# A row scale moved from the up products to the down products of a squared-ReLU MLP

## The chip, the cores and the metric

The kernel runs on one core of one Trainium2 chip. The core has a matrix engine (TensorE, PE in the profile; its weight loads are listed apart as PEld), VectorE (DVE), ScalarE (ACT), GpSimd (POOL), and SyncE (SP), which here only issues transfers. All five run their own instruction streams in order and wait for one another by semaphores. Matrix products land in PSUM, eight banks of 512 float32 per partition; everything else works in SBUF, 128 partitions wide. The metric is the device time of one execution in microseconds (us), lower is better.

## The reference

One layer of a streaming encoder on 512 tokens of width 1024, float32. After two attention-like blocks have been added to the residual `h`, the MLP and the final norm follow:

```
def rmsnorm(x, g):
    y = x * rsqrt(mean(x * x, axis=-1) + EPS)
    return y * g

u = rmsnorm(h, norm_ff_g) @ w1        # 1024 -> 4096
h = h + square(relu(u)) @ w2          # 4096 -> 1024
out = rmsnorm(h, final_norm_g)
```

The norm multiplies each token (row of `h`) by one positive number r and each feature by a gain. A positive factor per row passes through the product with `w1` and through relu, and comes out of the square as r squared; the product with `w2` keeps it as a factor of the row. So r may be applied on `u`, or r squared on the rows of the product with `w2`.

## The kernel before, in words

**Precision.** Every operand of a product is split into a high and a low part (`hi`, `lo`) by one ACT copy and one DVE subtraction, and each product runs as three: hi x hi, lo x hi, hi x lo (lines 240 to 242 for the up products, 1367 to 1369 for the down products). Weights come by transfer into raw buffers (`wr`, two of them, for the up weights; `wq` for the down weights), then ACT writes the high part (`whu`, `whd`, line 175) and DVE the low part (`wlu`, `wld`, line 179). Four buffers of each part rotate.

**Order of the work.** PE's order is written by hand: it is the program's order. The orders of ACT, DVE and POOL come from a planner that simulates the program by priority, which is program order, with weight splits put back by a fixed offset (`PW`). In the closing part (`last_product`) ACT and DVE are written by hand too.

**The residual before the MLP.** `residual` (line 1044) runs the output projection of the cross attention (`xw`) feature block by feature block, eight blocks of 128 features by 512 tokens. For each block DVE adds the product to the residual (`hT`), ACT and DVE write `x2_hi` and `x2_lo` with the gain applied (lines 1068 and 1069), and POOL squares the block and adds it to `ssq` (lines 1071 to 1075). Behind blocks 2, 4 and 6, and again in the MLP, `to_tok` transposes finished blocks on PE (`ht`, line 1167) and copies them into `acc`, four tiles of 128 tokens by 1024 features, to which the MLP's result is added.

**The MLP.** The 4096 hidden features go in eight groups of 512. For a group, `mlp_up` makes four tiles `u` of 128 hidden features by 512 tokens, 24 matmuls each, in PSUM banks that rotate among three (`mm`). `square` takes each: DVE computes `ur` = max(u, 0) times the row scale (line 1303, the scale broadcast to all partitions in `rbc`), and ACT squares it into `sq` (line 1306). `hidden_sums` (lines 1312 to 1315) forms sums and differences for a scheme of seven products in place of eight, and `hidden_part` splits those (`hb`). `mlp_down` runs the seven products in the order 1, 2, 6, 5, 7, 3, 4 into banks U, V, U, Y, U, Y, U, each twice, once for each half of the tokens. Bank U is accumulated further by products 6, 7 and 4, and bank Y by product 3, so that after each product the bank's present content is added to `acc` with a sign by `add_to` on DVE (lines 1333 and 1335) before PE may write it again. Down products of group g-1 run behind the up products of group g; the last down stretch takes groups 6 and 7 together. The last addition (line 1413) stands in `last_product`, in two halves of 256 columns.

**The scale before.** At the start of the MLP, after the first up tile, `mean_sq` sums `ssq` over the features on PE (`pm`, line 1085), POOL makes r by a power of -0.5, and after the second up tile PE broadcasts r over all partitions (`rbc`, line 1505), DVE copies it, and only then are the first two tiles squared:

```
    up0 = next(ups)
    ms2 = mean_sq(ssq2, "pm2")
    r2 = rstd_of(ms2, NT, "r2")
    to_tok(KC - 2)
    to_tok(KC - 1)
    up1 = next(ups)
```

Of the kernel before, what the change touches and what calls it, by code (L numbers as in the profile page):

```python
# [9 lines left out]
F32 = mybir.dt.float32  # L10
R = mybir.dt.float32r
U8 = mybir.dt.uint8
AF = mybir.ActivationFunctionType
ALU = mybir.AluOpType
AX = mybir.AxisListType

P = 128
S = 512
NT = S // P
D = 1024  # L20
KC = D // P
# [6 lines left out]
EPS = 1e-6  # L28
# [14 lines left out]
def emit(  # L43
# [22 lines left out]
    te, ve, ac, gp = nc.tensor, nc.vector, nc.scalar, nc.gpsimd  # L66
# [5 lines left out]
    cp = ctx.enter_context(tc.tile_pool(name="cp", bufs=1))  # L72
# [23 lines left out]
    def k4(shape, name, dt=F32):  # L96
        return k4p.tile([P] + shape, dt, tag="k4", name=name)
# [7 lines left out]
    def t2(name, dt=F32, shape=(S,)):  # L105
        return t2p.tile([P] + list(shape), dt, tag="t2", name=name)

    def sm(n, name):
        if n > 8:
            return s3p.tile([P, n], F32, tag="s3", name=name, padded_shape=[P, 32])  # L110
        return smp.tile([P, n], F32, tag="sm", name=name, padded_shape=[P, 8])
# [10 lines left out]
    def tr(name, shape=(S,)):  # L122
        return trp.tile([P] + list(shape), F32, tag="tr", name=name)
# [194 lines left out]
    ident = cp.tile([P, P], F32, name="ident")  # L318
# [24 lines left out]
    rows = t2("rows", F32, (P,))[0:33, :]  # L343
# [14 lines left out]
    def rstd_of(ms, n, name, r=None):  # L358

        e = sm(n, name + "e")  # L360
        gp.tensor_scalar(e, ms, 1.0, EPS, op0=ALU.mult, op1=ALU.add)
        if r is None:
            r = sm(n, name)
        gp.tensor_tensor(r, e, mhalf[:, 0:n], op=ALU.pow)
        return r
# [76 lines left out]
    with tc.manual_schedule(engines={mybir.EngineType.Activation, mybir.EngineType.DVE}):  # L442
# [66 lines left out]
        gf2 = gemm_fm(gfps[2], wt1, 0, hn_hi, hn_lo)  # L509
        for _ in range(GF):  # L510
            next(gf2)
        r0 = cp.tile([P, NT], F32, name="r0")
        rstd_of(ms0, NT, "r0", r0)

        fb = cp.tile([P, FH], F32, name="fb")
# [2 lines left out]
        pb = sc("rbc")  # L518
        for tb in range(NT):
            te.matmul(pb[:, tb * P : (tb + 1) * P], r0[:, tb : tb + 1].to_broadcast([P, P]), ident, start=True, stop=True)  # L520
        rbc = cp.tile([P, S], F32, name="rbc")
# [41 lines left out]
    g_x, g_mem, g_ff, g_h = gv[:, 0:8], gv[:, 8:16], gv[:, 16:24], gv[:, 24:25]  # L563
    gate(3)
    forget(3)
    for hp in range(2):
        wt = next_panel()
        for j in range(2):
            h = 2 * hp + j
            ps = mm(f"gq{h}")  # L570
# [124 lines left out]
    for li, m in enumerate(mlev):  # L695
# [8 lines left out]
        for hp in range(2):  # L704
# [3 lines left out]
            ps = sc(f"lv{hp}{m}", (NT, 2, w))  # L708
# [123 lines left out]
    for c in range(NT):  # L832
# [24 lines left out]
        with ahead(P1):  # L857
            hs = sm(4, f"hs{c}")
            for h in range(4):
                j = t2(f"hj{c}{h}", F32, (P,))  # L860
# [134 lines left out]
    for n in range(len(pairs) + 2):  # L995
        if n < len(pairs):
            p, tb = pairs[n]
# [46 lines left out]
    def residual(src_hi, src_lo, g, dst_hi, dst_lo, name, ssq, order, nlast, after=None):  # L1044

        ps_, gens = {}, {}

        def open_(c):
            if c % 2 == 0:
                open_.wt = next_panel()  # L1050
            ps_[c] = mm(f"{name}{c}")
            gens[c] = gemm_fm(ps_[c], open_.wt, (c % 2) * P, src_hi, src_lo, order=order)

        def early():

            for c in range(3):
                open_(c)
                for _ in range(KC - nlast):
                    yield next(gens[c])

        def rest():
            for c in range(KC):
                if c not in gens:
                    open_(c)
                yield from gens[c]
                hc = hTc(c)
                ve.tensor_tensor(hc, hc, ps_[c], ALU.add)  # L1067
                ac.activation(dst_hi[:, c, :], hc, AF.Identity, scale=g[:, c : c + 1])  # L1068
                ve.scalar_tensor_tensor(dst_lo[:, c, :], hc, g[:, c : c + 1], f(dst_hi[:, c, :]), op0=ALU.mult, op1=ALU.subtract)
                if c == 0:  # L1070
                    gp.tensor_tensor(ssq, hc, hc, op=ALU.mult)
                else:
                    sq = t2(f"{name}sq{c}")
                    gp.tensor_tensor(sq, hc, hc, op=ALU.mult)
                    gp.tensor_tensor(ssq, ssq, sq, op=ALU.add)
                if after is not None and c in (2, 4, 6):
                    after(c - 2)
                    after(c - 1)

        return early, rest  # L1080

    def mean_sq(ssq, name):
        pm = tr(name, (NT,))
        for tb in range(NT):
            te.matmul(pm[:, tb : tb + 1], ssq[:, tb * P : (tb + 1) * P], ones, start=True, stop=True)
        ms = sm(NT, name + "m")
        ve.tensor_scalar(ms, pm, 1.0 / D, None, op0=ALU.mult)
        return ms
# [8 lines left out]
    o_hi, o_lo = act_tile("o_hi"), act_tile("o_lo")  # L1097
# [14 lines left out]
    run_now(x_proj(0))  # L1112
    ms1 = mean_sq(ssq1, "pm1")
    r1 = rstd_of(ms1, NT, "r1")
    r16 = cp.tile([P, NT], F32, name="r16")
    gp.tensor_scalar(r16, r1, 1.0 / 16.0, 0.0, op0=ALU.mult, op1=ALU.add)

    def x_scores(h, tp):
# [43 lines left out]
    acc = []  # L1162
# [14 lines left out]
    for h in range(4):  # L1177
        if 0 < h < 3:
            fill.add(x_proj(h + 1), f"xq{h + 1}")
        elif h == 3:  # L1180
            x2_hi, x2_lo = act_tile("x2_hi"), act_tile("x2_lo")
            ssq2 = t2("ssq2")
            early, rest = residual(o_hi, o_lo, g_ff, x2_hi, x2_lo, "xw", ssq2, range(KC), 2, to_tok)
            fill.add(early())
        x_scores(h, 0)
        fill.run(X1)
        x_scores(h, 1)
        fill.run(X2 + X3)
        x_T_(h, 0)
        x_T_(h, 1)  # L1190
        pth, ptl = s4([2, S], f"pth{h}", R), s4([2, S], f"ptl{h}", R)
        for mc in range(2):
            ac.activation(pth[:, mc, :], xpT[h][mc], AF.Copy)
            ve.tensor_tensor(ptl[:, mc, :], xpT[h][mc], f(pth[:, mc, :]), ALU.subtract)
        if h < 3:
            fill.until(f"xq{h + 1}")
        else:
            fill.run(X4)
        x_out(h, pth, ptl)
# [99 lines left out]
            yield g, j, i, ps  # L1299

    def square(g, j, i, ps):
        u = t2(f"ur{g}{j}{i}")
        ve.scalar_tensor_tensor(u, ps, 0.0, rbc2, op0=ALU.max, op1=ALU.mult)  # L1303
        if i == 0:
            sqs[g, j] = k4([2, S], f"sq{g}{j}")
        ac.activation(sqs[g, j][:, i, :], u, AF.Square)  # L1306

    def hidden_sums(g):
        qa, qb = sqs[g, 0], sqs[g, 1]
# [18 lines left out]
        hbs[g, name] = hb  # L1328

    def add_to(ps, rows, half, t, sign):  # L1330
        a = acc[2 * rows + t][:, half * S : (half + 1) * S]
        if sign > 0:
            ve.tensor_tensor(a, ps, a, ALU.add)
        else:
            ve.scalar_tensor_tensor(a, ps, -1.0, a, op0=ALU.mult, op1=ALU.add)


    PLAN = {
# [42 lines left out]
    def last_product(gs, banks):  # L1381

        name = PRODUCTS[-1]

        def steps(g, t, cols):
            (whi, wlo), hb = unit("d", g, name), hbs[g, name]
            for k in range(2):
                hi, lo = (hb[:, x, k, t * P : (t + 1) * P] for x in range(2))
                yield from ((hi, whi[:, k, cols]), (hi, wlo[:, k, cols]), (lo, whi[:, k, cols]))

        def product(ps, t, cols, start):
            ops = [op for g in gs for op in steps(g, t, cols)]
            for i, (a, b) in enumerate(ops):
                te.matmul(ps, a, b, start=start and i == 0, stop=i == len(ops) - 1, skip_group_check=True)

        with tc.manual_schedule(engines={mybir.EngineType.Activation, mybir.EngineType.DVE}):
            add_to(banks["U", 1], 1, 0, 1, 1)
            product(banks["U", 0], 0, slice(0, S), False)
            add_to(banks["U", 0], 1, 0, 0, 1)
            o2, o3, v = s4([D], "fo2"), s4([D], "fo3"), fin[3][0]  # L1400
            _, half1, o1, r1_ = deferred
            scale_a(1, o1, r1_)
            e2 = sm(1, "fv2")
            ac.activation(o2[:, 0:S], acc[2][:, 0:S], AF.Square, scale=1.0 / 32.0, accum_out=e2)
            gp.tensor_tensor(e2, e2, fin[2][0], op=ALU.add)
            r2_ = row_scale(e2, "fr2")
            dma_a(1, o1)
            scale_b(1, half1, o1, r1_, gfin[half1])
            for q in range(2):
                qs = slice(q * HS, (q + 1) * HS)  # L1410
                ps = mm(f"Z{q}")[:, 0:HS]
                product(ps, 1, qs, True)
                ve.tensor_tensor(acc[3][:, qs], ps, acc[3][:, qs], ALU.add)
                v = squares(3, o3, qs, v, f"fv3{q}")
            for tb, o, r in ((2, o2, r2_), (3, o3, row_scale(v, "fr3"))):
                scale_a(tb, o, r)
                dma_a(tb, o)
                scale_b(tb, 0, o, r, gfin_ps)
# [73 lines left out]
    down_units((NG - 2, NG - 1))  # L1492
    order = [k for k, _ in unit_q]

    rbc2 = rbc
    ups = mlp_up_group(0)
    up0 = next(ups)
    ms2 = mean_sq(ssq2, "pm2")
    r2 = rstd_of(ms2, NT, "r2")
    to_tok(KC - 2)  # L1500
    to_tok(KC - 1)
    up1 = next(ups)
    pb = tr("rbc2")
    for tb in range(NT):
        te.matmul(pb[:, tb * P : (tb + 1) * P], r2[:, tb : tb + 1].to_broadcast([P, P]), ident, start=True, stop=True)
    ve.tensor_copy(rbc2, pb)
    square(*up0)
    square(*up1)
    for up in ups:
        square(*up)  # L1510
    hidden_sums(0)
# [43 lines left out]
```

## Time and profile before

| | |
|---|---|
| runs | 768.29, 768.75, 768.94 us (median 768.75) |
| profiled execution, first to last instruction | 766.8 us, the only time given for it |
| PE busy | 757.8 us, 99%, 4085 matmul instructions, clock granted in full |
| DVE busy | 525.2 us, 68% |
| ACT busy | 366.8 us, 48% |
| POOL busy | 193.6 us, 25% |
| MLP on PE | from 430.5 us to 759.9 us |

The profile is one execution. Its page gives the busy share of each engine and the chain of work that ended last, followed back from the last instruction to whatever released each step. The groups of instructions name line, engine, operation, output and inputs, shape and count; after the bar stand the busy time in us and the mean duration of one in ns, after the next bar the engine's idle time just before them and what ended it. The timeline gives for each instruction its start and duration in us, and in brackets the idle time before it and its releaser. The matmuls of PE overlap: one of 512 columns is listed with 0.39 us, but the next starts 0.23 us after it. An instruction of PE in full float32 shows as two, so that four transposes are listed as eight.

### The profile page before, as it was taken

How to read it: one execution, taken by the hardware profiler on the slowest of the kernel's cores; microseconds unless marked ns; L12 is line 12 of the kernel's file. 1: busy time of each engine (PE TensorE's matmuls, PEld its weight loads, DVE VectorE, ACT ScalarE, POOL GpSimd, SP SyncE). 2: the span in 40 equal slices, each digit the busy share in tenths (PEclk: the TensorE clock that was granted, in tenths of full speed). 3: DMA queues.
4: the chain of work that ended last, by engine and by line, in shares of the span. 5: the costliest groups of instructions: out<-in, count | busy, mean ns of one | idle time of the engine just before them, and what ended most of it. 6: DMA issues, size and time to landing. Idle time of an engine off the chain costs nothing.

```text
span 766.8 us, 10952 instructions
## 1 busy us (share of the span) xinstructions
PE 757.8 (99%) x4085; PEld 638.0 (83%) x4085; DVE 525.2 (68%) x848; ACT 366.8 (48%) x617; POOL 193.6 (25%) x264
## 2 busy tenths in 40 slices
PE   9999999999999999999999999999999999999996
PEld 6889888888889988888888888888888888888885
DVE  5747863678877656565548566949596877777696
ACT  5655554656666523344444344435353534343553
POOL 7207531322542225310016510101011010101123
PEclk9999999999999999999999999999999999999999
DMA  8541333313535432231113695575758475758602
GB/s 247 193 129 56 95 84 111 111 56 111 194 115 175 136 124 83 89 99 61 56 56 109 210 257 138 147 173 161 178 151 202 140 185 146 193 138 220 136 1 110
DMA packets 78870, 103.01 MB, mean 134 GB/s; under 512 B 4657, under 2 KB 56410, under 8 KB 78818
## 3 DMA queue, kind: packets, MB, share of 16 engines
q1 hardware_dynamic: 69266, 76.61, 31.2%
q0 software_dynamic: 8960, 24.67, 15.3%
q10 hardware_dynamic: 592, 1.05, 0.4%
q8 instruction: 32, 0.52, 0.3%
q14 instruction: 20, 0.16, 0.1%
HBM read 89.71 MB, written 4.21 MB: 122 GB/s over the span
## 4 chain that ended last, share of the span: by engine, by line
PE 95%; DVE 2%; ACT 1%; POOL 1%; issue 1%; ACTq 0%; POOLq 0%
PE u L241 8%; PE u L242 8%; PE u L240 8%; PE U L1368 4%; PE U L1369 4%; PE U L1367 4%; PE xq L240 2%; PE wo L240 2%; PE xq L241 2%; PE xw L240 2%; PE xq L242 2%; PE xw L241 2%; PE wo L241 2%; PE xw L242 2%; PE wo L242 2%; PE Y L1368 2%
## 5 line engine op out<-in xcount | busy, mean ns | idle before, releaser
L179 DVE TENSOR_TENSOR wld<-wq,whd 128x1024 fp32r<-128x1024 f32 x56 | 68.4, 1222 | 24.8 <-ACT whd L175 24.7
L240 PE MATMUL u<-x_hi,whu 128*128 128x512 f32 x192 | 74.7, 389 | 0.0
L241 PE MATMUL u<-x_lo,whu 128*128 128x512 f32 x192 | 74.7, 389 | 0.0
L242 PE MATMUL u<-x_hi,wlu 128*128 128x512 f32 x192 | 74.7, 389 | 0.0
L175 ACT ACTIVATE whd<-wq 128x1024 fp32r<-128x1024 f32 x56 | 58.4, 1052 | 30.5 <-PE u L241 21.6
L175 ACT ACTIVATE whu<-wru 128x1024 fp32r<-128x1024 f32 x24 | 25.3, 1053 | 61.2 <-DMA wru<-in_w_dram 61.2
L1243 POOL DMA_DIRECT2D wq<-in_w_dram x16 | 19.4, 1242 | 130.3 <-DMA wq<-in_w_dram 118.9
L179 DVE TENSOR_TENSOR wlu<-wru,whu 128x1024 fp32r<-128x1024 f32 x24 | 29.3, 1220 | 32.0 <-ACT whu L175 32.0
L1367 PE MATMUL U<-whd,hb 128*128 128x512 f32 x120 | 46.7, 389 | 0.0
L1368 PE MATMUL U<-wld,hb 128*128 128x512 f32 x120 | 46.7, 389 | 0.0
L1369 PE MATMUL U<-whd,hb 128*128 128x512 f32 x120 | 46.7, 389 | 0.0
L1243 POOL DMA_DIRECT2D wq<-wq x16 | 14.1, 878 | 122.7 <-DVE wld L179 95.9
L240 PEld LDWEIGHTS u<-x_hi,whu 128*128 128x128 f32 x192 | 36.0, 188 | 7.5
L241 PEld LDWEIGHTS u<-x_lo,whu 128*128 128x128 f32 x192 | 36.0, 188 | 7.5
L242 PEld LDWEIGHTS u<-x_hi,wlu 128*128 128x128 f32 x192 | 36.0, 188 | 7.4
L925 POOL TENSOR_SCALAR bi<-nF,Ft 128x128 f32<-128x128 f32 (+3 forms) x32 | 22.7, 718 | 58.2 <-PE pt L957 33.4
L1306 ACT ACTIVATE sq<-ur 128x512 f32<-128x512 f32 x32 | 20.0, 625 | 27.0 <-DVE ur L1303 27.0
L1303 DVE SCALAR_TENSOR_TENSOR ur<-u,rbc 128x512 f32<-128x512 f32 x32 | 21.9, 687 | 13.0 <-PE u L242 13.0
L1367 PEld LDWEIGHTS U<-whd,hb 128*128 128x128 f32 x120 | 22.5, 188 | 4.7
L1368 PEld LDWEIGHTS U<-wld,hb 128*128 128x128 f32 x120 | 22.5, 188 | 4.7
L1369 PEld LDWEIGHTS U<-whd,hb 128*128 128x128 f32 x120 | 22.5, 188 | 4.7
L1068 ACT ACTIVATE x_hi<-hT,gv 128x512 fp32r<-128x512 f32 x16 | 11.5, 716 | 30.4 <-DVE hT L1067 30.4
(961 smaller groups left out, 2311.7 us busy)
## 6 DMA issues: line engine op xcount, KB each, us to landing
wq<-in_w_dram SPq DMA_DIRECT2D x40, 512.0 KB, 3.3
wru<-in_w_dram SPq DMA_DIRECT2D x24, 512.0 KB, 6.7
wq<-in_w_dram POOLq DMA_DIRECT2D x16, 512.0 KB, 8.2
wq<-wq POOLq DMA_DIRECT2D x16, 512.0 KB, 4.7
xTd<-xT POOLq DMA_DIRECT2D x4, 512.0 KB, 3.3
nF<-Fd POOLq DMA_DIRECT2D x8, 256.0 KB, 3.8
hT<-xTd POOLq DMA_DIRECT2D x4, 512.0 KB, 5.6
xt<-in_x_dram SPq DMA_DIRECT2D x3, 512.0 KB
```

The lines of the kernel that those rows point to most:

```text
L175: ac.activation(hi, raw, AF.Copy)
L179: ve.tensor_tensor(lo, raw, f(hi), ALU.subtract)
L240: te.matmul(ps, wh, hi, start=n_ == 0 and not begun, stop=False)
L241: te.matmul(ps, wh, lo, start=False, stop=False)
L242: te.matmul(ps, wl, hi, start=False, stop=k == order[-1])
L925: gp.tensor_scalar(bi[:, 0:n], fF[h][:, 0:n], -1.0, Ft[:, tb, h : h + 1], op0=ALU.mult, op1=ALU.add)
L1243: gp.dma_start(raw.rearrange("p (k n) -> p k n", k=2), src, accum_op=ALU.add)
L1303: ve.scalar_tensor_tensor(u, ps, 0.0, rbc2, op0=ALU.max, op1=ALU.mult)
L1306: ac.activation(sqs[g, j][:, i, :], u, AF.Square)
L1367: te.matmul(ps, hi, whi[:, k, :], start=begin, stop=False, skip_group_check=True)
L1368: te.matmul(ps, hi, wlo[:, k, :], start=False, stop=False, skip_group_check=True)
L1369: te.matmul(ps, lo, whi[:, k, :], start=False, stop=k == 1, skip_group_check=True)
```

## The change

The row scale leaves the up products. `square` is now a Relu and a Square, both on ACT, with no scale. The product's contribution to `acc` is multiplied by the squared scale of its token row, positive or negative by the sign of the addition, in one DVE operation with a scalar per partition. The mean square comes from `acc` itself, where a token is a partition: ACT squares each of the four tiles and sums along the row, and DVE takes the reciprocal. POOL's squares in this residual, `mean_sq`'s matmuls, the broadcast on PE and its copy are gone; the other use of `residual` and `mean_sq`, ahead of the cross attention, stays. A small tile of the scale used in the cross attention (`r16`) moves into the tile of `r0`.

```
-        r0 = cp.tile([P, NT], F32, name="r0")
+        r0t = cp.tile([P, 2, NT], F32, name="r0")
+        r0, r16 = r0t[:, 0, :], r0t[:, 1, :]
...
-                if c == 0:
+                if ssq is None:
+                    pass
+                elif c == 0:
                     gp.tensor_tensor(ssq, hc, hc, op=ALU.mult)
...
-            ssq2 = t2("ssq2")
-            early, rest = residual(o_hi, o_lo, g_ff, x2_hi, x2_lo, "xw", ssq2, range(KC), 2, to_tok)
+            early, rest = residual(o_hi, o_lo, g_ff, x2_hi, x2_lo, "xw", None, range(KC), 2, to_tok)
...
     def square(g, j, i, ps):
-        u = t2(f"ur{g}{j}{i}")
-        ve.scalar_tensor_tensor(u, ps, 0.0, rbc2, op0=ALU.max, op1=ALU.mult)
         if i == 0:
             sqs[g, j] = k4([2, S], f"sq{g}{j}")
-        ac.activation(sqs[g, j][:, i, :], u, AF.Square)
+        u = sqs[g, j][:, i, :]
+        ac.activation(u, ps, AF.Relu)
+        ac.activation(u, u, AF.Square)
...
     def add_to(ps, rows, half, t, sign):
-        a = acc[2 * rows + t][:, half * S : (half + 1) * S]
-        if sign > 0:
-            ve.tensor_tensor(a, ps, a, ALU.add)
-        else:
-            ve.scalar_tensor_tensor(a, ps, -1.0, a, op0=ALU.mult, op1=ALU.add)
+        tb = 2 * rows + t
+        a = acc[tb][:, half * S : (half + 1) * S]
+        ve.scalar_tensor_tensor(a, ps, rsq[sign][:, tb : tb + 1], a, op0=ALU.mult, op1=ALU.add)
...
-                ve.tensor_tensor(acc[3][:, qs], ps, acc[3][:, qs], ALU.add)
+                ve.scalar_tensor_tensor(acc[3][:, qs], ps, rsq[1][:, 3:4], acc[3][:, qs], op0=ALU.mult, op1=ALU.add)
...
-    rbc2 = rbc
     ups = mlp_up_group(0)
-    up0 = next(ups)
-    ms2 = mean_sq(ssq2, "pm2")
-    r2 = rstd_of(ms2, NT, "r2")
+    square(*next(ups))
     to_tok(KC - 2)
     to_tok(KC - 1)
-    up1 = next(ups)
-    pb = tr("rbc2")
-    for tb in range(NT):
-        te.matmul(pb[:, tb * P : (tb + 1) * P], r2[:, tb : tb + 1].to_broadcast([P, P]), ident, start=True, stop=True)
-    ve.tensor_copy(rbc2, pb)
-    square(*up0)
-    square(*up1)
+    square(*next(ups))
+    ms2 = sm(NT, "ms2")
+    for tb in range(NT):
+        ac.activation(k4([D], f"sj{tb}"), acc[tb], AF.Square, scale=1.0 / 32.0, accum_out=ms2[:, tb : tb + 1])
+    rsqt = cp.tile([P, 2, NT], F32, name="rsq")
+    rsq = {1: rsqt[:, 0, :], -1: rsqt[:, 1, :]}
+    e2 = sm(NT, "r2e")
+    gp.tensor_scalar(e2, ms2, 1.0, EPS, op0=ALU.mult, op1=ALU.add)
+    ve.reciprocal(rsq[1], e2)
+    ve.tensor_scalar(rsq[-1], rsq[1], -1.0, None, op0=ALU.mult)
```

More of the change, by code (lines that the diff above doesn't have):

```diff
@@ L1114, in emit @@
     r1 = rstd_of(ms1, NT, "r1")
-    r16 = cp.tile([P, NT], F32, name="r16")
     gp.tensor_scalar(r16, r1, 1.0 / 16.0, 0.0, op0=ALU.mult, op1=ALU.add)
```

## The prediction

> **What bounds the kernel now.** I read the page first, its busy shares and the chain that ended last:
>
> ```profile
> span 766.8 us, 10952 instructions
> PE 757.8 (99%) x4085; PEld 638.0 (83%) x4085; DVE 525.2 (68%) x848; ACT 366.8 (48%) x617; POOL 193.6 (25%) x264
> ...
> PE 95%; DVE 2%; ACT 1%; POOL 1%; issue 1%; ACTq 0%; POOLq 0%
> ```
>
> TensorE (PE) is busy for 99% and makes 95% of the chain: only PE time removed, PE time added, or a new PE wait can move the end. The sum below is made against this execution's 766.8 us; the median of the three runs, 768.75, stands 1.95 above it, and I carry differences over unchanged.
>
> Next, the table of stretches, for one MLP period: down products of one group (first row), then up products of the next (second row).
>
> ```profile
> 517.51:536.55 19.04, 19.04 (x86) 15.77 (x84) 18.67 (x27) 10.12 (x13) 2.01 (x2) 1.00 0.52 161
> 536.55:558.31 21.76, 21.76 (x98) 18.02 (x96) 11.91 (x14) 7.53 (x10) 2.17 (x3) 1.00 0.71 168
> ```
>
> After the total come PE, weight loads, VectorE (DVE), ScalarE (ACT), GpSimd (POOL), each with its count. PE is full in both, at full clock. DVE is full in the down stretch too (18.67 of 19.04) and half idle in the up stretch. So DVE is the engine to watch: work added to it among the down products can become a PE wait. Six such down stretches follow one another before the closing one of groups 6 and 7.
>
> Third, the chain in order of time, where the norm's own PE work stands:
>
> ```profile
> 424.33 0.87 PE ht L1167 x8
> ...
> 436.11 0.79 PE pm L1085 x8
> 436.90 0.93 PE ht L1167 x8
> ...
> 443.30 0.89 PE rbc L1505 x8
> ...
> 759.94 0.44 DVE acc L1413
> ```
>
> **The change part by part.** *Matmuls removed.* The mean-square matmuls (pm) take 0.79 us on the chain, the broadcast of the row scale (rbc) 0.89; each is four products, shown as eight instructions. The transposes behind pm take 0.93 where the same eight take 0.87 elsewhere, so 0.06 more should go. Sum: 0.79 + 0.06 + 0.89 = 1.74 us off PE. The lower end is 0.79 + 0.79 = 1.58, if the slower restart inside the 0.89 and the 0.06 stay. Nothing takes their place on PE: the transposes need only the residual and a free bank, and the up products run on.
>
> *Squares of the residual removed from POOL*: fifteen operations, all of POOL's work in the stretch of the output projection:
>
> ```profile
> 398.00:436.00 38.00, 38.00 (x183) 31.67 (x181) 29.25 (x35) 15.20 (x27) 22.61 (x15) 1.00 0.35 112
> ```
>
> That is 22.61 us of POOL (the last engine of the row), beside a PE that waits for none of it: counted as nothing. With it goes the small POOL and DVE work of the old scale, equally covered.
>
> *Mean square by ACT*, and the relu moved from DVE to ACT. Rows of like forms:
>
> ```profile
> L1303 DVE SCALAR_TENSOR_TENSOR ur<-u,rbc 128x512 f32<-128x512 f32 x32 | 21.9, 687 | 13.0 <-PE u L242 13.0
> L1306 ACT ACTIVATE sq<-ur 128x512 f32<-128x512 f32 x32 | 20.0, 625 | 27.0 <-DVE ur L1303 27.0
> L1159 ACT ACTIVATE o_hi<-xo 128x512 fp32r<-128x512 f32 x8 | 4.8, 595 | 3.6 <-PE xo L1158 3.5
> L435 ACT ACTIVATE x0j<-xt 128x1024 f32<-128x1024 f32 x2 | 2.1, 1057 | 0.0
> L435 ACT ACTIVATION_READ_ACCUMULATOR x0j<-xt 128x1 f32 x2 | 0.4, 197 | 0.0
> ```
>
> Four row squares of 1057 ns with an accumulator read of 197 are 5.0 us of ACT, just after the last transposes are copied, about 439 to 444. They push back the split of the next weight panel, and the new POOL, DVE pair behind them makes the scale at about 445:
>
> ```profile
> 438.47 2.54 POOL L1243 DMA_DIRECT2D wq<-in_w_dram  x2
> 440.44 1.06 ACT L175 ACTIVATE wh36a<-wr36a 128x1024 fp32r<-128x1024 f32 x1 [1.66 <-PE u L241]
> 454.95 0.39 PE L240 MATMUL u<-x_hi,wh36a 128*128 128x512 f32 x1
> 479.52 0.68 DVE L1333 TENSOR_TENSOR acc<-U,acc 128x512 f32<-128x512 f32 x1
> ```
>
> PE reaches that panel at 454.95, by 1.7 less afterwards; even a start of the split at 445 leaves some 5 us for it and its DVE half. The scale is first used at 479.52. The reciprocal is a new wait on DVE, for POOL's small add; queued behind it are the panel's low halves. If POOL issues its two DMAs (2.54) first, the wait grows by that, still inside the 5 us. Cost nothing; without that cover at most 5 us, once.
>
> In each group four DVE operations of 687 go and four Relu on ACT come. The nearest row is ACT's copy out of PSUM, 595, shorter than what it replaces. ACT rises by 4 x 0.595 = 2.4 us to 9.9 of 21.76 in the up stretch: no bound. The PSUM bank of an up product is freed by ACT instead of DVE, with three banks in rotation. This move has one tight place. Where the down products start, ACT runs thus:
>
> ```profile
> 517.48 1.06 ACT L175 ACTIVATE whd<-wq 128x1024 fp32r<-128x1024 f32 x1 [1.66 <-PE u L241]
> 518.45 0.62 ACT L1306 ACTIVATE sq<-ur 128x512 f32<-128x512 f32 x1
> ```
>
> and on DVE at the same time:
>
> ```profile
> 518.58 1.23 DVE L179 TENSOR_TENSOR wld<-wq,whd 128x1024 fp32r<-128x1024 f32 x1 [0.17 <-ACT whd L175]
> 519.72 0.68 DVE L1312 TENSOR_TENSOR s<-sq,sq 128x512 f32<-128x512 f32 x1
> ```
>
> Relu at 518.45 and Square behind it end at about 518.45 + 0.595 + 0.625 = 519.67; DVE is in its weight split until 519.72 anyway. So the sums start when they did: cost nothing, with no slack to spare.
>
> The Trainium skill speaks against this move: "ScalarE: Activation LUTs", in its rules for kernel authors, sends relu to VectorE and calls VectorE up to about three times as fast per element in bf16. Here the data is float32 out of PSUM and the two rows above say the reverse, 595 against 687; read as three times 687 the Relu would be 2.06 us, an estimate from that page, and by the third rival's working the sum would end at 773.1 in place of the one below.
>
> *The scale at the joins.* Each addition becomes a scalar_tensor_tensor with a scalar per partition. Trace rows, without and with such a scalar, one input in PSUM:
>
> ```profile
> L1335 DVE SCALAR_TENSOR_TENSOR acc<-U,acc 128x512 f32<-128x512 f32 x28 | 17.9, 679 | 0.0
> L1333 DVE TENSOR_TENSOR acc<-U,acc 128x512 f32<-128x512 f32 x28 | 18.5, 681 | 0.4 <-PE U L1394 0.4
> L816 DVE SCALAR_TENSOR_TENSOR mx_lo<-pr,gv,mx_hi 128x512 fp32r<-128x512 f32 x4 | 3.0, 742 | 0.0
> L890 DVE SCALAR_TENSOR_TENSOR mel<-mnt,gv,meh 128x256 fp32r<-128x256 f32 x8 | 3.8, 476 | 0.0
> L1413 DVE TENSOR_TENSOR acc<-Z,acc 128x256 f32<-128x256 f32 x2 | 0.8, 424 | 0.6 <-PE Z L1394 0.5
> ```
>
> So +0.063 us each (742 - 679), fourteen per down stretch, +0.88 on a full engine. Where it could stop PE is the reuse of bank U by the last product, and behind that the last weight unit of the next up products (DVE's timeline, then PE's):
>
> ```profile
> 532.12 1.28 DVE L1335 SCALAR_TENSOR_TENSOR acc<-U,acc 128x512 f32<-128x512 f32 x2
> ...
> 547.74 1.23 DVE L179 TENSOR_TENSOR wlu<-wru,whu 128x1024 fp32r<-128x1024 f32 x1 [3.18 <-ACT whu L175]
> 533.83 0.39 PE L1367 MATMUL U<-whd,hb 128*128 128x512 f32 x1
> ...
> 550.60 0.39 PE L242 MATMUL u<-x_hi,wlu 128*128 128x512 f32 x1
> ```
>
> The first addition of the pair ends at 532.12 + 0.68 = 532.80, 1.03 before PE needs the bank. Eight additions stand ahead of it since 520: with its own, 9 x 0.063 = 0.57, leaving 0.46. The last unit ends at 548.97, 1.63 before its use; its load waits for a buffer freed behind twelve additions, 0.76, leaving 0.87. Cost nothing.
>
> At the very end the last addition, 128 x 256, lies on the chain: 476 - 424 = +0.05 us there, between 0 and 0.1.
>
> **Sum**: -1.74 + 0.05 = -1.69 us, the span to 765.1, the median to 767.06: -0.22%. A measurement can tell about 0.2% (1.54 us) from no change, so the forecast stands just past that edge.
>
> **The rivals.** *First: the additions use up the slack.* For: DVE falls behind PE in every down stretch, and 0.46 is little. Against: the scalar's price is steady over rows of two widths. If each addition costs 0.1 more than I take, nine make 0.9, less 0.46 is 0.44 of PE wait, six times 2.6: 769.7. Half that excess just spends the slack. I place it between: 768.4.
>
> *Second: the removed matmuls only uncover a wait.* If the transposes, now 0.8 earlier, wait for a bank or for the last residual tile, only the rbc part is won: -0.89 + 0.05, 767.9. Against: the same transposes at 424.33 have no pm ahead of them, and the chain goes into them from PE without a wait.
>
> *Third, on the other side: the sums start late.* ScalarE's order is the planner's. If Relu and Square stand behind one more weight split (1.06, row at 517.48), or take that much longer, s and all additions behind it slip by 1.06. PE then waits 1.06 - 0.46 = 0.60 in each of six down stretches, 3.6 us: 770.7, slower. It decides from a slip of 0.46 + 1.69 / 6 = 0.74 us. For: no slack at 519.72. Against: ACT is busy 10.12 of 19.04 us there, and the same queue served the Square in time before. A Relu slower than its row would act in this way; that part of the chance is 0.02. It is what the page's rule on relu would do; the rows contradict it so far.
>
> *Fourth: Relu swaps ACT's function table.* A swap costs:
>
> ```profile
> L545 ACT ACT_TABLE_LOAD x1 | 1.3, 1283 | 0.0
> ```
>
> Two swaps for each of 32 tiles put 2.6 us between a product and its Square; by the third rival's sum the slip is 2.6 - 0.46 = 2.1 in six stretches, 12.8 us: 780. For: no row here runs Relu. Against: Copy, Identity and Square share one table all through the MLP, where no load stands. The same page of the Trainium skill, section "Table sets: the hidden batching unit", holds that relu is a filler in every set; no run here shows it yet, and by it this rival falls away.
>
> **How the numbers follow.** Forecast 0.67; first rival 0.13; second 0.05; third 0.13; fourth 0.02. The forecast's own range is 766.5 (lowest run 768.29 less 1.74, the tail at nothing) to 767.6 (lower end of the PE gain, 0.1 at the tail, 0.3 of scatter). The edge, 767.21, cuts it: about seven tenths lie below. Faster: 0.67 x 0.7 = 0.47. Slower: third, fourth and the top of the first, 0.17. The rest, 0.36, is the same. The range 766.5 to 769.6 leaves out the third and fourth rivals and little else.
>
> **What would show it.** Right: no pm and rbc in the chain; eight-instruction transposes at 0.87; Relu near 595 on ACT without table loads; additions near 742; 4 row squares near 1057 ending before 446; PE full in the six down stretches, each 19.04 long. Wrong: a down stretch longer than 19.04 with PE waiting for DVE acc (first or third rival, told apart by when s starts), ACT table loads in the MLP, or a PE gap in front of the last transposes or of panel 36.

## The result and the profile after

| | before | after |
|---|---|---|
| median of 8 runs each, one session (range), us | 768.30 (768.07 to 768.94) | 766.18 (765.79 to 766.97) |
| span of the profiled execution, us | 766.8 | 764.3 |

The ratio is 0.9974, with a 95% interval from 0.9964 to 0.9984. The profiled run of the changed kernel took 766.06 us. Against the median of three runs shown before, 768.75, the gain is 2.57 us; against the eight runs beside it, 2.12. The prediction was 767.06, with a range that began at 766.5: the time lies 0.3 below the range, although every gain on PE came out where it was forecast.

The page of the changed kernel, its span, busy shares and the engines' shares of the chain:

```profile
span 764.3 us, 10886 instructions
PE 755.3 (99%) x4069; PEld 635.5 (83%) x4069; DVE 502.8 (66%) x816; ACT 388.6 (51%) x657; POOL 170.3 (22%) x248
...
PE 95%; DVE 2%; ACT 1%; POOL 1%; issue 1%; ACTq 0%; POOLq 0%
```

PE lost 2.5 us of busy time and sixteen instructions (eight of pm, eight of rbc). POOL lost 23.3, ACT gained 21.8, and PE is still the bound.

The table of stretches of the changed kernel, the same columns as in the prediction: the output projection, then the second down stretch and the up stretch behind it:

```profile
398.00:436.00 38.00, 38.00 (x186) 31.78 (x185) 21.57 (x35) 15.89 (x29) 0.00 (x0) 1.00 0.37 119
...
514.97:534.01 19.04, 19.04 (x85) 15.77 (x84) 17.97 (x25) 10.70 (x14) 1.47 (x2) 1.00 0.55 160
534.01:555.77 21.76, 21.76 (x97) 18.02 (x96) 10.82 (x12) 9.20 (x13) 2.71 (x3) 1.00 0.73 174
```

The down stretch still takes 19.04 us and PE is full in it: no new wait. In the chain of the changed kernel there is no pm and no rbc, the last transposes run at their usual length, and the last addition is longer:

```profile
435.37 0.87 PE ht L1169 x8
...
757.40 0.49 DVE acc L1412
```

The groups of the changed kernel, for the operations that the change added or altered:

```profile
L1334 DVE SCALAR_TENSOR_TENSOR acc<-U,rsq,acc 128x512 f32<-128x512 f32 x56 | 39.8, 744 | 0.3 <-PE U L1393 0.3
L1307 ACT ACTIVATE sq<-sq 128x512 f32<-128x512 f32 x32 | 20.2, 633 | 1.0
L1306 ACT ACTIVATE sq<-u 128x512 f32<-128x512 f32 x32 | 18.7, 584 | 20.5 <-PE u L242 20.5
L1501 ACT ACTIVATE sj<-acc 128x1024 f32<-128x1024 f32 x4 | 4.2, 1051 | 0.0
```

A join takes 744 ns, a Relu out of PSUM 584, a row square 1051. The load of a function table stands nowhere in the MLP.

**Where the time went.** I compared the starts of the same matmuls on PE's timeline, the first up product `u` and the first product `Z` of the closing part. Before:

```profile
430.50 0.39 PE L240 MATMUL u<-x_hi,wh34a 128*128 128x512 f32 x1
...
756.87 0.28 PE L1394 MATMUL Z<-whd,hb 128*128 128x256 f32 x1
```

After:

```profile
429.75 0.39 PE L240 MATMUL u<-x_hi,wh34a 128*128 128x512 f32 x1
...
754.33 0.28 PE L1393 MATMUL Z<-whd,hb 128*128 128x256 f32 x1
```

From `u` to `Z` are 326.37 us before and 324.58 after: 1.79 us gained in the MLP. From `Z` to the issue of the last output transfer (762.30 and 759.82 on the timeline) are 5.43 and 5.49: 0.06 lost. The other 0.75 was there before the MLP began, and nearly all of it before the first real product. PE's timeline in the first 7 us, before:

```profile
4.73 1.12 PE L412 MATMUL xn<-ident,xt 128*128 128x128 f32 x4
5.64 1.60 PE L447 MATMUL warm<-zero 128*128 128x512 bf16 x4
6.89 0.59 PE L458 MATMUL gf<-hn_hi,wh0a 128*128 128x512 f32 x1
```

and after:

```profile
4.73 0.66 PE L412 MATMUL xn<-ident,xt 128*128 128x128 f32 x4
5.23 1.03 PE L447 MATMUL warm<-zero 128*128 128x512 bf16 x4
6.17 0.73 PE L458 MATMUL gf<-hn_hi,wh0a 128*128 128x512 f32 x2
```

Four transposes of the first input tile take 0.66 us in place of 1.12, the four warm-up matmuls `warm` behind them 1.03 in place of 1.60, and the first matmul `gf` starts 0.72 us earlier. (A transpose is listed as one instruction: the eight of `ht` are those of two blocks, and it is the full-float32 products of pm and rbc that show as two each.) The change touches no instruction there; the order on every engine is the same up to the output projection. Late input isn't the reason either: the transposes start at 4.73 in both profiles, and the warm-up matmuls read only a tile of zeros. PE itself ran more slowly: taken one by one, the first warm-up matmuls start 0.43 us apart before (5.64, 6.07, 6.49) and 0.22 after (5.23, 5.44, 5.66). The trace's record of the granted TensorE clock says the same: it turns full at 6.80 us before and at 4.71 after. So 2.5 us of span are 0.72 (start), 0.03 (up to `u`), 1.79 (MLP) and -0.06 (tail).

### The profile page after: what moved, and what is told of

It reads as the page before. It is cut to its first block, busy times and chain, and to the rows that moved or that the text cites. A ratio compares the mean times of both kernels' runs of the same rounds, so it can differ in the third digit from the quotient of the medians.

```text
span 764.3 us, 10886 instructions
## 1 busy us (share of the span) xinstructions
PE 755.3 (99%) x4069; PEld 635.5 (83%) x4069; DVE 502.8 (66%) x816; ACT 388.6 (51%) x657; POOL 170.3 (22%) x248
## 4 chain that ended last, share of the span: by engine, by line
PE 95%; DVE 2%; ACT 1%; POOL 1%; issue 1%; ACTq 0%; POOLq 0%
PE u L240 8%; PE u L241 8%; PE u L242 8%; PE U L1366 4%; PE U L1367 4%; PE U L1368 4%; PE xq L240 2%; PE wo L240 2%; PE xq L241 2%; PE xq L242 2%; PE xw L241 2%; PE xw L242 2%; PE wo L242 2%; PE xw L240 2%; PE wo L241 2%; PE Y L1366 2%
## 5 line engine op out<-in xcount | busy, mean ns | idle before, releaser
L1334 DVE SCALAR_TENSOR_TENSOR acc<-U,rsq,acc 128x512 f32<-128x512 f32 x56 | 39.8, 744 | 0.3 <-PE U L1393 0.3
L1306 ACT ACTIVATE sq<-u 128x512 f32<-128x512 f32 x32 | 18.7, 584 | 20.5 <-PE u L242 20.5
L1324 ACT ACTIVATE hb<-s 128x512 fp32r<-128x512 f32 x24 | 15.0, 629 | 20.6 <-PE U L1368 13.6
```

What stands on the lines that cost most here:

```text
L1306: ac.activation(u, ps, AF.Relu)
L1334: ve.scalar_tensor_tensor(a, ps, rsq[sign][:, tb : tb + 1], a, op0=ALU.mult, op1=ALU.add)
```

## The experiments

My theory after this result: the change is worth its two removed PE operations, 1.74 us, and the additions, Relu and row squares cost PE nothing; the further 0.7 us of span are scatter of the start. Rivals: the moved `r16` changed the layout and so the start; the move of the Relu or the POOL squares gave or cost something of their own; the additions stand at the edge of their slack and already cost some of the gain. For each kernel I took, beside its times, two distances on PE from its profile: first `gf` to first `u`, and first `u` to first `Z`, which leave the start out.

**The two kernels again**, without an edit.

> The kernel before, unchanged, timed against itself and profiled once more. Theory A (the first microseconds scatter from run to run): a ratio of 1.000 within 0.0005, and a profile in which the first matmul of the first projection (gf) starts anywhere between 6.1 and 6.9 us, while the stretch from there to the start of the MLP is as long as in the first profile within 0.1 us. Theory B (the start belongs to the kernel): gf starts at 6.9 again.

> The changed kernel, unchanged, for a second profile and a tighter ratio. Theory A: 1.75 us below the kernel before plus or minus the scatter of the start (ratio 0.9972 to 0.9982), gf starting anywhere between 6.1 and 6.9. Theory B (the start is faster by some 0.4 to 0.7 us in this kernel for a reason of its own): gf at 6.2 again, 2.1 to 2.5 us below, ratio 0.9967 to 0.9973.

> The kernel before once more, for the start: where its first projection begins in another profile, and the scatter of its times. If the start only scatters: gf between 6.1 and 7.0 us, and the median of its times less the start's place in the profile agrees with the other two profiles of it.

> The changed kernel once more, for the start and for the ratio: if the start scatters alike in both kernels, about 1.75 us below the kernel before in these rounds; if its start is earlier by nature, 2.1 again with gf before 6.6.

Measured: the kernel before took 768.45 and 768.28, each even with the runs beside it (1.0001, interval 0.9992 to 1.0010; 0.9998, 0.9989 to 1.0007). The changed kernel took 766.46 beside 768.61 (0.9976, 0.9966 to 0.9986) and 766.50 beside 768.37 (0.9974, 0.9964 to 0.9983). The gains are 2.15 and 1.87. The distances repeat to a hundredth where the start doesn't:

| profile | clock full at | first `gf` at | `gf` to `u` | `u` to `Z` | span |
|---|---|---|---|---|---|
| before | 6.80 | 6.89 | 423.61 | 326.37 | 766.8 |
| same_before | 5.42 | 6.48 | 423.51 | 326.37 | 766.3 |
| second_before | 6.87 | 6.93 | 423.62 | 326.37 | 766.8 |
| after | 4.71 | 6.17 | 423.58 | 324.58 | 764.3 |
| same_after | 5.58 | 6.56 | 423.53 | 324.58 | 764.7 |
| second_after | 6.09 | 6.63 | 423.47 | 324.58 | 764.7 |

It follows that the MLP's gain is 1.79 in every execution profiled, and that the same program starts between 6.17 and 6.63, or between 6.48 and 6.93. A single pair of profiles can show 0.7 us that the change didn't make. The later the clock turns full, the later `gf` starts. That holds over twelve of the fourteen profiles of this case, from 4.18 and 6.05 us (`tiny`) to 7.06 and 6.99 (`r16_only`); in the other two, `pe_back` and `dve_relu`, `gf` waited 0.49 and 0.16 us for its weights.

**The layout of `r16` alone.** The kernel before, with `r16` in the tile of `r0`:

```
-        r0 = cp.tile([P, NT], F32, name="r0")
+        r0t = cp.tile([P, 2, NT], F32, name="r0")
+        r0, r16 = r0t[:, 0, :], r0t[:, 1, :]
...
-    r16 = cp.tile([P, NT], F32, name="r16")
```

> One part alone: the kernel before with only the small scale tile r16 moved into the tile of r0; every engine's order is that of before. Theory A: as before, ratio 1.000 within 0.0005. Theory B, with the layout of the tiles as the reason: 0.4 to 0.7 us faster, ratio 0.9991 to 0.9995, gf at 6.2.

Measured 768.40 beside 768.61, 0.9998 (0.9990 to 1.0007); `gf` at 6.99, `u` to `Z` 326.37. This part of the change does nothing.

**The two PE operations put back.** The changed kernel with four matmuls like pm and four like rbc, whose results nothing reads:

```
     square(*next(ups))
+    pm = tr("pm2", (NT,))
+    for tb in range(NT):
+        te.matmul(pm[:, tb : tb + 1], hTc(0)[:, tb * P : (tb + 1) * P], ones, start=True, stop=True)
     to_tok(KC - 2)
     to_tok(KC - 1)
     square(*next(ups))
+    pb = tr("rbc2")
+    for tb in range(NT):
+        te.matmul(pb[:, tb * P : (tb + 1) * P], r0[:, tb : tb + 1].to_broadcast([P, P]), ident, start=True, stop=True)
```

> One part undone: the changed kernel with the eight matmuls put back on TensorE where they stood, four like pm and four like rbc, on other data and with results that nobody reads; nothing else waits for them. My account of the sum (all of the gain is the matmuls' own time): 1.74 us slower than the changed kernel, so within 0.1 us of the kernel before where the start scatters alike. Rival (part of the gain is that waits or queues behind the scale went): less than 1.2 us slower than the changed kernel.

Measured 768.42 beside 768.61, 1.0000 (0.9991 to 1.0009): all of the gain is gone. The chain of this kernel has the rows of before:

```profile
435.76 0.79 PE pm L1498 x8
436.55 0.93 PE ht L1169 x8
...
442.95 0.89 PE rbc L1504 x8
```

`u` to `Z` is 326.75, 2.17 above the changed kernel. Some 0.34 of that is a stall of another kind, in this one profile. PE's timeline there, then ACT's:

```profile
669.70 0.39 PE L241 MATMUL u<-x_lo,whu 128*128 128x512 f32 x1
670.16 0.50 PE L242 MATMUL u<-x_hi,wlu 128*128 128x512 f32 x1
670.50 0.40 PE L240 MATMUL u<-x_hi,whu 128*128 128x512 f32 x1
```

```profile
667.79 1.06 ACT L175 ACTIVATE whu<-wru 128x1024 fp32r<-128x1024 f32 x1 [11.08 <-DMA wru<-in_w_dram]
```

Matmuls start 0.23 apart; here the steps are 0.46 and 0.34. A weight panel landed late, so its split came late, and PE waited for the low half. The rest, 1.83, is what the sum gives for the two operations (1.74 and restarts).

**The mean square by POOL and PE kept.** The changed kernel, but with POOL's squares and the pm matmuls of before in place of the row squares:

```
-            early, rest = residual(o_hi, o_lo, g_ff, x2_hi, x2_lo, "xw", None, range(KC), 2, to_tok)
+            ssq2 = t2("ssq2")
+            early, rest = residual(o_hi, o_lo, g_ff, x2_hi, x2_lo, "xw", ssq2, range(KC), 2, to_tok)
...
+    ms2 = mean_sq(ssq2, "pm2")
...
-    for tb in range(NT):
-        ac.activation(k4([D], f"sj{tb}"), acc[tb], AF.Square, scale=1.0 / 32.0, accum_out=ms2[:, tb : tb + 1])
```

> Half of the change: the scale goes to the joins and the broadcast (rbc) is gone, but the mean square still comes from POOL's squares and the four matmuls pm on TensorE. My account: 0.79 + 0.06 = 0.85 us of the gain is missing, so 0.9 us below the kernel before (ratio 0.9988 less or more the scatter of the start, 0.9980 to 0.9992), and in the profile the transposes behind pm take 0.93. Rival (POOL's 22.6 us beside DVE also cost something): more than 1.2 us is missing.

Measured 767.29 beside 768.41, 0.9986 (0.9977 to 0.9995). `u` to `Z` is 325.44, which is 0.86 above the changed kernel: pm's 0.79 and 0.06 or 0.07 behind it. Half of the change's gain is the mean square's way, half the broadcast's. `gf` to `u` is 423.58, as without the squares: POOL's 22.6 us in the output projection, and what they cost DVE there (last section), delay PE by nothing.

**The Relu on DVE, without a scale.**

```
-        ac.activation(u, ps, AF.Relu)
-        ac.activation(u, u, AF.Square)
+        ur = t2(f"ur{g}{j}{i}")
+        ve.tensor_scalar(ur, ps, 0.0, None, op0=ALU.max)
+        ac.activation(u, ur, AF.Square)
```

> One part undone: the relu stays on DVE (a maximum with zero, no scale, into the old intermediate tile), ACT squares it; all else as in the changed kernel. My account (the move to ACT is worth nothing either way, PE waits for neither): the same time as the changed kernel within 0.3 us, PE full in all six down stretches. Rival (the move to ACT is part of the gain): more than 0.5 us slower than the changed kernel.

Measured 766.63 beside 768.41, 0.9977 (0.9968 to 0.9985); `u` to `Z` 324.58. The down stretch of this kernel:

```profile
515.20:534.24 19.04, 19.04 (x85) 15.77 (x84) 18.66 (x26) 10.12 (x13) 1.41 (x2) 1.00 0.54 159
```

DVE works 18.66 of 19.04 us there, 0.69 more than with the Relu on ACT, and PE doesn't notice. The engine of the Relu is worth nothing here.

**The joins without the scale.** The additions of before, so that this kernel leaves the row scale out of them:

```
-        ve.scalar_tensor_tensor(a, ps, rsq[sign][:, tb : tb + 1], a, op0=ALU.mult, op1=ALU.add)
+        if sign > 0:
+            ve.tensor_tensor(a, ps, a, ALU.add)
+        else:
+            ve.scalar_tensor_tensor(a, ps, -1.0, a, op0=ALU.mult, op1=ALU.add)
```

> The joins as before, additions and subtractions without the scale, so that this kernel leaves the row scale of the MLP out (except in the last two half tiles); all else as in the changed kernel. My account (the scale at the joins costs nothing on TensorE): within 0.1 us of the changed kernel from the start of the first projection to the end, each addition back at 0.68 us. Rival (the slower additions took back part of the gain): 0.5 us or more below the changed kernel.

Measured 766.25 beside 768.37, 0.9971 (0.9960 to 0.9983); `u` to `Z` 324.58. Its group of additions:

```profile
L1335 DVE TENSOR_TENSOR acc<-U,acc 128x512 f32<-128x512 f32 x28 | 18.6, 689 | 0.4 <-PE U L1396 0.4
```

689 in place of 744 ns, and the same time: the scale at the joins is hidden, as forecast.

**How much slack is left?** Three kernels push the additions later. `late1` repeats one subtraction of 0.60 us ahead of the sums, `late2` does it twice:

```
+        for _ in range(1):
+            ve.tensor_tensor(s7, A2b, A2a, ALU.subtract)
         ve.tensor_tensor(s5, A2b, A2a, ALU.subtract)
```

> The slack measured: the changed kernel with one more DVE subtraction (0.60 us each, result overwritten) ahead of the sums of every group, so that all additions of a down stretch come 0.60 us later. My account: bank U is free 0.47 us before the last product in the changed kernel, so PE waits 0.13 in each of six down stretches, 0.8 us in all. Rival (the slack is larger, PE waits elsewhere): no difference. Rival (the slack was already used up): 6 x 0.6 = 3.6 us slower than the changed kernel.

> The same with two such subtractions, 1.20 us: my account 6 x (1.20 - 0.47) = 4.4 us slower than the changed kernel, with down stretches of 19.8 us in place of 19.04, and so some 2.6 us slower than the kernel before. Rival (larger slack): less than 2 us. Rival (slack used up): 7.2 us.

Measured 769.00 beside 768.41 for the first (1.0007, 0.9998 to 1.0016) and 774.87 for the second (1.0086, 1.0070 to 1.0101). `u` to `Z` rose by 2.40 and 8.33 us over the changed kernel, where 0.8 and 4.4 had been expected. In `late1` the loss sits at two places of each of the six stretches, 0.2 at each: in front of product 6, and in front of the last product. DVE's timeline of `late1` at the two places, then PE's:

```profile
519.99 0.74 DVE L1336 SCALAR_TENSOR_TENSOR acc<-U,rsq,acc 128x512 f32<-128x512 f32 x1
...
531.07 1.40 DVE L1336 SCALAR_TENSOR_TENSOR acc<-U,rsq,acc 128x512 f32<-128x512 f32 x2
```

```profile
520.57 0.39 PE L1370 MATMUL V<-whd,hb 128*128 128x512 f32 x1
520.88 0.47 PE L1368 MATMUL U<-whd,hb 128*128 128x512 f32 x1
521.18 0.39 PE L1369 MATMUL U<-wld,hb 128*128 128x512 f32 x1
...
531.96 0.47 PE L1368 MATMUL U<-whd,hb 128*128 128x512 f32 x1
```

The additions end at 519.99 + 0.74 = 520.73 and 531.07 + 0.74 = 531.81; PE's matmuls into the freed bank start at 520.88 and 531.96. So 0.15 us pass from the end of DVE's row to PE's start. And the waiting matmul is followed after 0.30 where others are after 0.23: a further 0.07 or 0.08 for each wait. The view of waits lists none of this.

The first of the two places isn't in the prediction at all. The planner moved the early additions behind more of the sums: in `late1` three sums and the added subtraction stand ahead of the first addition, in the changed kernel one sum (517.19, with the addition at 517.80, next section). `late2` shows it larger. Its view of waits, then DVE's timeline and PE's:

```profile
PE U L1368 <- DVE acc L1336: 6.7, 6, 1.1
```

```profile
522.17 0.68 DVE L1317 TENSOR_TENSOR s<-n,sq 128x512 f32<-128x512 f32 x1
522.77 1.40 DVE L1336 SCALAR_TENSOR_TENSOR acc<-U,rsq,acc 128x512 f32<-128x512 f32 x2
```

```profile
523.66 0.47 PE L1368 MATMUL U<-whd,hb 128*128 128x512 f32 x1 [1.12 <-DVE acc L1336]
```

Both additions stand behind all the sums, and PE waits six times. These two kernels thus mix a delay with a new order. The third leaves the sums alone and lengthens every join by a small copy from its bank:

```
+        ve.tensor_copy(sm(8, "tiny"), ps[:, 0:8])
         ve.scalar_tensor_tensor(a, ps, rsq[sign][:, tb : tb + 1], a, op0=ALU.mult, op1=ALU.add)
```

> The first rival's price, with the order of the additions kept: a DVE copy of 8 columns out of the product's bank ahead of every addition, some 0.08 to 0.09 us each by the rows of like copies (165 ns less the overlap of 0.08). Nine of them make 0.77 ahead of the last product's bank. By the slack of 0.32 that the kernels with late sums showed (0.47 between the two rows, less 0.15 from the end of an addition to the start of the matmul) and 0.08 for each restart: 6 x (0.77 - 0.32 + 0.08) = 3.2 us slower than the changed kernel, all of it in front of the last product of each down stretch. By the slack of 0.46 as predicted: 6 x 0.31 = 1.9 us. If PE does not wait for the additions: nothing.

Measured 770.07 beside 768.37, 1.0021 (1.0012 to 1.0030), slower than before; `u` to `Z` rose by 2.92, six times 0.49, all in front of the last product. The planner moved the first two additions here too, behind one and two more sums, but PE lost nothing in front of product 6. In the closing part the last addition comes 3.73 us behind `Z`, against 3.07 in the changed kernel: 0.66 more. Together that is nearly the 3.57 us between this kernel and the changed one of the same session (766.50), where 3.2 had been expected, all of it in front of the last products. Its view of waits, DVE's timeline and PE's:

```profile
PE U L1367 <- DVE tiny L1334: 1.2, 6, 0.2
```

```profile
531.07 0.75 DVE L1335 SCALAR_TENSOR_TENSOR acc<-U,rsq,acc 128x512 f32<-128x512 f32 x1
```

```profile
531.38 0.39 PE L1369 MATMUL Y<-whd,hb 128*128 128x512 f32 x1
531.96 0.47 PE L1367 MATMUL U<-whd,hb 128*128 128x512 f32 x1 [0.19 <-DVE tiny L1334]
532.27 0.40 PE L1368 MATMUL U<-wld,hb 128*128 128x512 f32 x1
```

Counted from the first `u` of each kernel (429.55 here), and less the 0.49 of the stretch before, this addition starts 0.70 later than the same one in the changed kernel (530.08, next section). 0.70 less 0.32 of slack is 0.38, plus 0.08 for the restart 0.46, near the 0.49 measured. The copies lengthen a join by 0.08 (530.99 to 531.07 on DVE's timeline). So about 0.08 us more on every join turns the change into a loss.

## Why the prediction was wrong at its edge and right about PE

**The matmuls removed: right.** Forecast 1.74, measured 1.79 from `u` to `Z`. Along the aligned starts, 0.81 goes at pm, 0.05 at the transposes behind it, 0.81 at rbc and 0.09 at the restart behind that, 1.76 in all; 0.03 is spread over the matmuls that follow. The lower end, 1.58 with the slower restarts kept, did not come; the second rival (only rbc won) fell, since the transposes follow their predecessor without a gap.

**POOL's squares at nothing: right**, by `pm_kept`.

**The mean square by ACT: right, a little early.** ACT's timeline of the changed kernel, then DVE's:

```profile
441.30 0.19 ACT L1501 ACTIVATION_READ_ACCUMULATOR sj<-acc 128x1 f32 x1
441.39 1.05 ACT L175 ACTIVATE wh36a<-wr36a 128x1024 fp32r<-128x1024 f32 x1
```

```profile
441.81 0.18 DVE L1506 RECIPROCAL rsq<-r2e 128x4 f32<-128x4 f32 x1 [3.11 <-POOL r2e L1505]
...
442.47 1.23 DVE L179 TENSOR_TENSOR wl36a<-wr36a,wh36a 128x1024 fp32r<-128x1024 f32 x1 [0.28 <-ACT wh36a L175]
```

I forecast the end of the row squares at 444 and the scale at 445; they came at 441.5 and 442.0, of which 0.75 is the earlier start of this execution. DVE did wait for POOL, 3.11 us, and the low half of panel 36 still ended some 9 us before PE reached it.

**The Relu on ACT at nothing: right**, and the third rival (sums start late) fell. ACT's timeline where the down products start, then DVE's:

```profile
515.91 0.58 ACT L1306 ACTIVATE sq<-u 128x512 f32<-128x512 f32 x1
516.52 0.63 ACT L1307 ACTIVATE sq<-sq 128x512 f32<-128x512 f32 x1
```

```profile
517.19 0.69 DVE L1313 TENSOR_TENSOR s<-sq,sq 128x512 f32<-128x512 f32 x1
517.80 0.75 DVE L1334 SCALAR_TENSOR_TENSOR acc<-U,rsq,acc 128x512 f32<-128x512 f32 x1
```

Counted from the start of the stretch, `s` begins at 517.19 - 514.97 = 2.22 us; before it was 519.72 - 517.51 = 2.21. The Relu at 584 ns beat both my 595 and the 687 of the DVE operation it replaced, so the reading of the Trainium skill ("ScalarE: Activation LUTs", section "Rules for kernel authors") as three times 687 is out; `dve_relu` adds that the engine doesn't matter here. The rival's point of decision, however, was wrong: I put it at a slip of 0.74, and `late1` lost 2.40 us, more than the gain, at a slip of 0.60.

**The fourth rival fell.** No table is loaded in the MLP of the changed kernel. That agrees with the Trainium skill, "ScalarE: Activation LUTs", section "Table sets: the hidden batching unit", by which relu is a filler in every set.

**The joins at nothing: right, but with less to spare than I said.** Forecast 742 ns each and 0.46 left in front of the last product; measured 744, and DVE's row, then PE's:

```profile
530.08 1.40 DVE L1334 SCALAR_TENSOR_TENSOR acc<-U,rsq,acc 128x512 f32<-128x512 f32 x2
```

```profile
531.29 0.39 PE L1366 MATMUL U<-whd,hb 128*128 128x512 f32 x1
```

The gap between the rows is 531.29 - 530.08 - 0.74 = 0.47, as forecast. But a gap between rows isn't all slack: less the 0.15 from DVE's end to PE's start, 0.32 is usable. The first rival (additions use up the slack) names the mechanism that `tiny` shows, at the place and six times as it said; the scalar's price simply stayed where the rows had it. The margin was 0.32 us, or about 0.04 for each of nine additions.

**The tail: right.** 0.05 forecast, 0.06 measured; the last addition takes 0.49 in place of 0.44.

**The step that failed is the range's low end**, "766.5 (lowest run 768.29 less 1.74, the tail at nothing)", and two terms behind it were mis-sized. The measured 766.18 lies 0.88 under the forecast of 767.06: 0.45 of that is the base (768.75 against the 768.30 beside the changed kernel), 0.43 the gain (2.12 against 1.69).

*The base* took three runs for the whole scatter of the kernel before. Over the later runs that kernel goes from 767.70 to 769.05, and its medians in four sessions are 768.30, 768.61, 768.41 and 768.37, some 0.3 under the 768.75 that I subtracted from. In the profiles the span moves with the start: `gf` starts between 6.05 and 6.99 over all fourteen, mostly as the clock of PE turns full earlier or later, while the distance from there to `u` is 423.47 to 423.66 in thirteen of them (423.88 in `late2`, where PE waited 0.18 for an input tile at 8.7 us and slipped again at about 11.6). Lowest run 767.70 less 1.74 is 765.96 for a single run, and the mean of the later medians, 768.42, less 1.69 is 766.73 for the median.

*The gain* on the engines was right: the forecast of the sum, -1.69, was 0.04 off what the aligned rows show (1.79 less 0.06). What failed is "I carry differences over unchanged", from the span to the time 1.95 above it. That distance isn't the same in both kernels. In the two later sessions that timed both, the mean time stands 1.96 and 1.88 above the mean span in the kernel before, and 1.73 and 1.72 in the changed one. So 0.23 and 0.16 us of the gain lie outside the span, where the prediction put nothing.

**What stays open.** The measured gains, 2.12, 2.15 and 1.87, are all above the 1.73 that the rows account for. The four profiles with the program of before (`r16_only` among them) start `gf` at 6.82 on average, the ten of the changed kernel and its variants at 6.43. The spans of all runs speak against a start that belongs to the program: the mean span fell by 1.71 and 1.72 us in those two sessions (each known to some 0.1), as the rows say, with nothing left for the start. The rest is what lies outside the span, before the first instruction or behind the last. It goes with the changed program and not with PE's work: the distance is 1.70 to 1.73 in `pe_back`, `pm_kept`, `dve_relu`, `late1`, `tiny` and `plain_joins` too (1.84 in the four runs of `late2`), and 1.91 in `r16_only`. Which part of the change makes it, and how, isn't shown. The intervals of the ratios, 0.9964 to 0.9984, hold 1.73 us (0.9977).

## What to carry to other kernels

Where PE is 99% busy, the rows of PE instructions in the chain that a change removes are its worth, and an engine relieved elsewhere adds nothing; the sum from such rows held here to 0.04 us. Slack read as the gap between two rows is too large by the handoff between the engines, and a delay of 0.6 us in a scheduled stream can cost more than its length, since the planner's order moves with it: test slack by lengthening the operations themselves, and see whether the order stayed. For differences near 0.2%, compare starts of the same instruction between profiles rather than spans, take the base and its scatter from more than three runs, and don't count on the time outside the span to stay as it was.

## What the runs showed of the hardware that was not expected

- PE's start after a wait for DVE: 0.15 us after the end of DVE's row (520.73 to 520.88, 531.81 to 531.96), and the second matmul follows after 0.30 or 0.31 in place of 0.23.
- The granted clock of PE turns full at different times in executions with the same instructions at that place, between 4.18 and 7.06 us over fourteen profiles. Until then the warm-up matmuls start 0.43 us apart, afterwards 0.22. The first matmul `gf` scatters by up to 0.94 us (6.05 to 6.99), and nothing behind makes it up.
- The time outside the span differs between programs: 1.96 and 1.88 us on average in the kernel before, 1.73 and 1.72 in the changed one.
- One transfer landed late, in one of fourteen profiles: in `pe_back` a panel's split began at 667.79 after 11.08 us of waiting, and cost PE 0.34 us.
- POOL's squares slowed DVE. The same DVE operation, in the stretch of the output projection, by the groups of before:

```profile
L1069 DVE SCALAR_TENSOR_TENSOR x_lo<-hT,gv,x_hi 128x512 fp32r<-128x512 f32 x8 | 10.2, 1278 | 1.3 <-ACT x_hi L1068 1.3
```

and of the changed kernel:

```profile
L1070 DVE SCALAR_TENSOR_TENSOR x_lo<-hT,gv,x_hi 128x512 fp32r<-128x512 f32 x8 | 6.0, 749 | 1.3 <-ACT x_hi L1069 1.3
```

1278 ns beside POOL's squares, 749 without, and 1278 again in `pm_kept`, where they are back. That agrees with the Trainium skill, "GPSIMD Engine Reference", section "Specifications", by which POOL contends with DVE instructions that have two SBUF inputs, as this one has. DVE's busy time in that stretch fell from 29.25 to 21.57 us; PE gained nothing from it, since it waited for none of it.
